# ReLU and row sum on one core: the last row in two halves instead of three pieces, and a closing wait on the two engines without work

## The chip, the core and the metric

The kernel runs on one core of a Trainium2 chip. The core has five engines that each run their own stream of instructions: TensorE (PE), VectorE (DVE), ScalarE (ACT), GpSimd (POOL) and SyncE (SP). They meet only at semaphores. SP issues the DMAs here, which 16 DMA engines carry out. The metric is the device time of one execution in microseconds (us), the median of several runs.

## The reference

The input is 32 x 512 rows of 1024 float32 numbers, 67.1 MB. Each number is clipped at zero from below, and each row is summed:

```python
def reference(x):                       # x: 32 x 512 x 1024, float32
    relu_x = np.maximum(x, 0)
    return np.sum(relu_x, axis=-1).astype(np.float32)
```

So 16,384 sums come out, 64 KB.

## The kernel before, in words

The 16,384 rows are spread over 128 partitions, 128 rows to each. The rows of the first region (112 a partition) are loaded as seven chunks of 16 rows, 8.4 MB each; the second region (16 a partition) is the tail. Three buffers of 16 rows a partition (`buf`) take the chunks in turn; the tail goes into the buffer that is next in turn. All sums gather in `res`, one column for each row of a partition.

There are two ways to take a row's sum:

- In chunks 0 to 5, ACT clips a group of 4, 5 or 7 rows in place (L119) and DVE sums that group in one reduction (L121). In chunk 5 the groups are 3, 4 and 5 rows, and the other four rows are taken in the second way.
- One instruction clips and sums a row by itself: `on_act` (L99) on ACT or `on_dve` (L102) on DVE. Each is followed by a small instruction that reads the accumulated sum out. Chunk 6 and the tail are done so, row by row in alternation, both engines at once.

SP's stream sets the order of the loads. It issues chunk after chunk (L73); from the fourth on it first waits for DVE to be done with the buffer that is to be filled. When the last buffer is free, it issues the tail without a wait in between: 8, 4, 2 and 1 rows (L79), and then the last row of each partition in three column pieces, 576, 256 and 192 wide (L87). Each load has a semaphore of its own (`s_in`). Then SP waits for the sums of chunk 6 (L90, L91) and stores the first region's 112 columns (L93). All of this is one queue in order.

The last row is summed in parts. ACT takes the 576 columns and puts their sum into an extra column at the end of the small tile `last` (L148). DVE takes the 256 columns and puts their sum into a second extra column (L150). The third piece was loaded into `last` itself, so that one pass over 194 columns, 192 of the row and the two sums, gives the row's total (L154). Ahead of it DVE waits for the third piece and for both sums (L151 to L153). SP waits for that pass, stores the last 16 columns (L158) and waits for both stores (L159, L160).

TensorE and GpSimd have no work. Their streams hold only the program's start: an opening barrier of all engines and, on GpSimd, four small fills of constants (shown as L174).

Of the kernel before, what the change touches and what calls it, by code (L numbers as in the profile page):

```python
# [2 lines left out]

P = 128
D = 1024
BIG = 16
NTWO = 6
NB = 3
REGIONS = [112, 16]
CHUNKS = [(0, 0), (0, 16), (0, 32), (0, 48), (0, 64), (0, 80), (0, 96)]  # L10
STEPS = [4, 5, 7]
MIXED = [3, 4, 5]
TAIL = [8, 4, 2, 1]
LAST = [576, 256, 192]


def bass_relu_sum_kernel(
    nc: bass.Bass,
    x: bass.AP,
    out: bass.AP,  # L20
):

    fp32 = mybir.dt.float32
    ALU = mybir.AluOpType  # L30
    AF = mybir.ActivationFunctionType
    X = mybir.AxisListType.X

    B, S, _ = x.shape
    J = B * S // P
    NBIG = len(CHUNKS)
    assert BIG * NBIG + sum(TAIL) + 1 == J == sum(REGIONS) and sum(LAST) == D

    xr = x.rearrange("b s d -> (b s) d")
    of = out.rearrange("b s -> (b s)")  # L40
    start = [sum(REGIONS[:i]) for i in range(len(REGIONS))]
    xv = [
        xr[P * s : P * (s + n), :].rearrange("(p j) d -> p j d", p=P)
        for s, n in zip(start, REGIONS)
    ]
    ov = [of[P * s : P * (s + n)].rearrange("(p j) -> p j", p=P) for s, n in zip(start, REGIONS)]

    buf = nc.alloc_sbuf_tensor("buf", [P, NB, BIG, D], fp32)
    last = nc.alloc_sbuf_tensor("last", [P, LAST[2] + 2], fp32)
    res = nc.alloc_sbuf_tensor("res", [P, J], fp32)  # L50

    n_in = NBIG + len(TAIL) + len(LAST)
    s_in = [nc.alloc_semaphore(f"s_in{i}") for i in range(n_in)]
    s_act = nc.alloc_semaphore("s_act")
    s_dve = nc.alloc_semaphore("s_dve")
    s_fact = nc.alloc_semaphore("s_fact")
    s_fdve = nc.alloc_semaphore("s_fdve")
    s_tact = nc.alloc_semaphore("s_tact")
    s_tpart = nc.alloc_semaphore("s_tpart")
    s_tdve = nc.alloc_semaphore("s_tdve")  # L60
    s_store = nc.alloc_semaphore("s_store")
    s_out = nc.alloc_semaphore("s_out")

    sp, act, dve = nc.sync, nc.scalar, nc.vector


    tb = NBIG % NB
    for c in range(NBIG + 1):
        if c >= NB:
            sp.wait_ge(s_dve, 3 * (c - NB + 1))  # L70
        if c < NBIG:
            g, j = CHUNKS[c]
            sp.dma_start(out=buf[:, c % NB, :, :], in_=xv[g][:, j : j + BIG, :]).then_inc(  # L73
                s_in[c], 16
            )
    r = 0
    tail = []
    for i, n in enumerate(TAIL):
        sp.dma_start(out=buf[:, tb, r : r + n, :], in_=xv[-1][:, r : r + n, :]).then_inc(  # L79
            s_in[NBIG + i], 16  # L80
        )
        tail.append((r, n, s_in[NBIG + i]))
        r += n
    n0, n1 = LAST[0], LAST[0] + LAST[1]
    parts = [buf[:, tb, r, 0:n0], buf[:, tb, r, n0:n1], last[:, 0 : LAST[2]]]
    for k, (lo, hi) in enumerate([(0, n0), (n0, n1), (n1, D)]):
        sp.dma_start(out=parts[k], in_=xv[-1][:, BIG - 1, lo:hi]).then_inc(  # L87
            s_in[NBIG + len(TAIL) + k], 16
        )
    sp.wait_ge(s_fact, 1)  # L90
    sp.wait_ge(s_fdve, 1)  # L91
    for g in range(len(REGIONS) - 1):
        sp.dma_start(  # L93
            out=ov[g][:, :], in_=res[:, start[g] : start[g] + REGIONS[g]]
        ).then_inc(s_store, 16)


    def on_act(t, acc):
        return act.activation(t, t, AF.Relu, accum_out=acc)  # L99

    def on_dve(t, acc):
        return dve.tensor_scalar(  # L102
            out=t, in0=t, scalar1=0.0, scalar2=None, op0=ALU.max, op1=ALU.add, accum_out=acc
        )

    def row(c, i):
        return buf[:, c % NB, i, :], res[:, c * BIG + i : c * BIG + i + 1]

    for c in range(NTWO):
        b, steps = c % NB, STEPS if c < NTWO - 1 else MIXED  # L110
        act.wait_ge(s_in[c], 16)
        if steps is MIXED:
            dve.wait_ge(s_in[c], 16)
            for i in (BIG - 4, BIG - 3):
                on_dve(*row(c, i))
        r = 0
        for i, n in enumerate(steps):
            t = buf[:, b, r : r + n, :]
            act.activation(t, t, AF.Relu).then_inc(s_act, 1)  # L119
            dve.wait_ge(s_act, 3 * c + i + 1)  # L120
            dve.tensor_reduce(  # L121
                out=res[:, c * BIG + r : c * BIG + r + n], in_=t, axis=X, op=ALU.add
            ).then_inc(s_dve, 1)
            r += n
        if steps is MIXED:
            for i in (BIG - 2, BIG - 1):
                on_act(*row(c, i))


    j0 = NBIG * BIG  # L130
    for c in range(NTWO, NBIG):
        act.wait_ge(s_in[c], 16)
        dve.wait_ge(s_in[c], 16)
        for i in range(BIG):
            ins = (on_act if i % 2 else on_dve)(*row(c, i))
            if i >= BIG - 2:
                ins.then_inc(s_fact if i % 2 else s_fdve, 1)
    for r, n, s in tail:
        if n > 1:
            act.wait_ge(s, 16)  # L140
        dve.wait_ge(s, 16)
        for i in range(r, r + n):
            f = on_act if (i - r) % 2 else on_dve
            f(buf[:, tb, i, :], res[:, j0 + i : j0 + i + 1])

    n = LAST[2]
    act.wait_ge(s_in[-3], 16)
    on_act(parts[0], last[:, n : n + 1]).then_inc(s_tact, 1)  # L148
    dve.wait_ge(s_in[-2], 16)
    on_dve(parts[1], last[:, n + 1 : n + 2]).then_inc(s_tpart, 1)  # L150
    dve.wait_ge(s_in[-1], 16)  # L151
    dve.wait_ge(s_tpart, 1)
    dve.wait_ge(s_tact, 1)  # L153
    on_dve(last[:, :], res[:, J - 1 : J]).then_inc(s_tdve, 1)  # L154


    sp.wait_ge(s_tdve, 1)
    sp.dma_start(out=ov[-1][:, :], in_=res[:, start[-1] : J]).then_inc(s_out, 16)  # L158
    sp.wait_ge(s_store, 16 * (len(REGIONS) - 1))  # L159
    sp.wait_ge(s_out, 16)  # L160


# [1 line left out]
_INS = ['x']  # L164
_OUTS = [((32, 512), 'float32')]


# [21 lines left out]
```

## Time and profile before

| | before |
|---|---|
| median of 5 runs | 161.98 us (161.84 to 162.05) |
| the profiled execution | 161.84 us |
| its span, first to last instruction | 160.5 us |
| DVE busy | 122.0 us, 76% |
| ACT busy | 101.0 us, 63% |
| POOL busy | 0.2 us; PE has no work |
| DMA, mean over the span | 419 GB/s |
| share of the chain that ended last | DMA 69%, ACT 18%, DVE 11%, SP's queue 1% |

A page of the profile shows one execution. The span is counted from the first to the last instruction of the kernel; the execution's time is longer by what lies around it. The chain of work that ended last is followed back from the last instruction, step by step, to whatever released it. In the timeline a row has its start, its duration, the engine (a q behind it means the engine's sequencer, which issues DMAs and waits), the line, the operation and the shapes; in brackets stands how long the engine had been idle before, and what ended that. The DMA issues give for each load its size and the time from the issue to its landing. Besides, the trace holds the times at which semaphores were updated, and the start, size and duration of each DMA packet.

### The profile page before, as it was taken

What the parts mean: (1) busy time and instruction counts of PE and PEld (TensorE: products, weight loads), DVE (VectorE), ACT (ScalarE), POOL (GpSimd) and SP (SyncE); (2) the same over time, 40 slices, a digit from 0 to 9 for tenths busy, and PEclk for the clock granted to TensorE, in tenths of its full rate; (3) what the DMA queues carried; (4) which work ended last, traced back from release to release, by engine and by line L of the source; (5) the groups of instructions that cost most, each with busy time, mean ns of one, the idle gap of its engine ahead of it and who ended that gap; (6) DMA issues with size and microseconds to landing.
All of it is one profiled execution on the core that took longest, in us unless ns stands there. A gap on an engine that the chain in (4) does not pass through costs nothing.

```text
span 160.5 us, 148 instructions
## 1 busy us (share of the span) xinstructions
DVE 122.0 (76%) x58; ACT 101.0 (63%) x55; POOL 0.2 (0%) x4
## 2 busy tenths in 40 slices
DVE  0000004998969898898969989699899999598995
ACT  3000039991599907997099951999329980496972
POOL 0000000000000000000000000000000000000000
DMA  7969969969969969969969969969969979799993
GB/s 261 523 278 506 523 261 523 523 261 523 523 261 523 523 261 523 523 261 523 523 261 523 523 261 523 523 261 523 506 278 523 457 327 523 343 441 388 412 402 123
DMA packets 2305, 67.18 MB, mean 419 GB/s; under 512 B 512, under 2 KB 768, under 8 KB 1024
## 3 DMA queue, kind: packets, MB, share of 16 engines
q1 hardware_dynamic: 2304, 67.18, 97.5%
q14 instruction: 1, 0.01, 0.0%
HBM read 67.11 MB, written 0.07 MB: 419 GB/s over the span
## 4 chain that ended last, share of the span: by engine, by line
DMA 69%; ACT 18%; DVE 11%; SPq 1%; issue 0%; DVEq 0%
DMA buf<-in_x_dram 69%; ACT buf L119 18%; DVE res L121 10%; DVE buf L102 1%; SPq L79 1%; SPq L73 0%; DVE last L102 0%; DVEq L153 0%
## 5 line engine op out<-in xcount | busy, mean ns | idle before, releaser
L121 DVE TENSOR_REDUCE res<-buf 128x4 f32<-128x4096 f32 (+3 forms) x18 | 100.4, 5604 | 34.2 <-ACT buf L119 34.2
L119 ACT ACTIVATE buf<-buf 128x4096 f32<-128x4096 f32 (+3 forms) x18 | 80.8, 4553 | 47.0 <-DMA buf<-in_x_dram 47.0
L99 ACT ACTIVATE buf<-buf 128x1024 f32<-128x1024 f32 (+1 forms) x18 | 18.4, 1024 | 9.8 <-DMA buf<-in_x_dram 9.8
L102 DVE TENSOR_SCALAR_CACHE_REDUCE buf<-buf 128x1024 f32<-128x1024 f32 (+1 forms) x19 | 21.3, 1174 | 2.7 <-DMA buf<-in_x_dram 2.5
L99 ACT ACTIVATION_READ_ACCUMULATOR buf<-buf 128x1 f32 x18 | 3.4, 187 | 0.0
L119 ACT ACT_TABLE_LOAD x1 | 1.3, 1283 | 0.7 <-PEq L174 0.7
L102 DVE DVE_READ_ACCUMULATOR buf<-buf 128x1 f32 x19 | 1.6, 83 | 0.0
L102 DVE TENSOR_SCALAR_CACHE_REDUCE last<-last 128x194 f32<-128x194 f32 x1 | 0.4, 355 | 0.1
L174 POOL MEMSET const-bfloat16-1.0<- 128x1 bf16 x1 | 0.1, 101 | 0.0
L174 POOL MEMSET const-uint8-127<- 128x1 uint8 x1 | 0.1, 101 | 0.0
L174 POOL MEMSET const-float32-0.0<- 128x1 f32 x1 | 0.1, 98 | 0.2 <-issue 0.2
L174 POOL MEMSET const-float32-1.0<- 128x1 f32 x1 | 0.1, 98 | 0.0
L102 DVE DVE_READ_ACCUMULATOR last<-last 128x1 f32 x1 | 0.1, 83 | 0.0
## 6 DMA issues: line engine op xcount, KB each, us to landing
buf<-in_x_dram SPq DMA_DIRECT2D x1, 4096.0 KB, 26.7
buf<-in_x_dram SPq DMA_DIRECT2D x1, 2048.0 KB, 31.2
buf<-in_x_dram SPq DMA_DIRECT2D x1, 1024.0 KB, 33.2
buf<-in_x_dram SPq DMA_DIRECT2D x1, 512.0 KB, 34.0
buf<-in_x_dram SPq DMA_DIRECT2D x1, 288.0 KB, 34.3
buf<-in_x_dram SPq DMA_DIRECT2D x1, 128.0 KB, 34.1
buf<-in_x_dram SPq DMA_DIRECT2D x7, 36.3
last<-in_x_dram SPq DMA_DIRECT2D x1, 96.0 KB, 33.9
```

Of the source, the lines that this page charges most:

```text
L79: sp.dma_start(out=buf[:, tb, r : r + n, :], in_=xv[-1][:, r : r + n, :]).then_inc(s_in[NBIG + i], 16)
L99: return act.activation(t, t, AF.Relu, accum_out=acc)
L102: return dve.tensor_scalar(out=t, in0=t, scalar1=0.0, scalar2=None, op0=ALU.max, op1=ALU.add, accum_out=acc)
L119: act.activation(t, t, AF.Relu).then_inc(s_act, 1)
L121: dve.tensor_reduce(out=res[:, c * BIG + r : c * BIG + r + n], in_=t, axis=X, op=ALU.add).then_inc(s_dve, 1)
L174: nc = _bacc.Bacc("TRN2", target_bir_lowering=False, num_devices=1)
```

## The change

The last row now arrives in two column pieces of 512 instead of three. ACT takes the first half and puts its sum behind the second half, in the one extra column of `last`; DVE's last pass goes over 513 columns. DVE's own pass over 256 columns, its sum and the semaphore `s_tpart` are gone. Of the two waits that are left ahead of the last pass, the one for ACT's sum now stands before the one for the load. At the end of their streams TensorE and GpSimd wait for the semaphore of the last load. Everything up to the last row is as it was.

```diff
-LAST = [576, 256, 192]
+LAST = [512, 512]
...
-    last = nc.alloc_sbuf_tensor("last", [P, LAST[2] + 2], fp32)
+    last = nc.alloc_sbuf_tensor("last", [P, LAST[1] + 1], fp32)
...
-    n0, n1 = LAST[0], LAST[0] + LAST[1]
-    parts = [buf[:, tb, r, 0:n0], buf[:, tb, r, n0:n1], last[:, 0 : LAST[2]]]
-    for k, (lo, hi) in enumerate([(0, n0), (n0, n1), (n1, D)]):
-        sp.dma_start(out=parts[k], in_=xv[-1][:, BIG - 1, lo:hi]).then_inc(
-            s_in[NBIG + len(TAIL) + k], 16
-        )
+    sp.dma_start(out=buf[:, tb, r, 0 : LAST[0]], in_=xv[-1][:, BIG - 1, 0 : LAST[0]]).then_inc(
+        s_in[-2], 16
+    )
+    sp.dma_start(out=last[:, 0 : LAST[1]], in_=xv[-1][:, BIG - 1, LAST[0] : D]).then_inc(
+        s_in[-1], 16
+    )
...
+    for idle in (nc.tensor, nc.gpsimd):
+        idle.wait_ge(s_in[-1], 16)
...
-    n = LAST[2]
-    act.wait_ge(s_in[-3], 16)
-    on_act(parts[0], last[:, n : n + 1]).then_inc(s_tact, 1)
-    dve.wait_ge(s_in[-2], 16)
-    on_dve(parts[1], last[:, n + 1 : n + 2]).then_inc(s_tpart, 1)
-    dve.wait_ge(s_in[-1], 16)
-    dve.wait_ge(s_tpart, 1)
-    dve.wait_ge(s_tact, 1)
+    act.wait_ge(s_in[-2], 16)
+    on_act(buf[:, tb, BIG - 1, 0 : LAST[0]], last[:, LAST[1] : LAST[1] + 1]).then_inc(s_tact, 1)
+    dve.wait_ge(s_tact, 1)
+    dve.wait_ge(s_in[-1], 16)
     on_dve(last[:, :], res[:, J - 1 : J]).then_inc(s_tdve, 1)
```

## The prediction

> **What bounds the kernel now.** I read the chain of work that ended last first, then the timeline of the last 4 us, then the DMA issues, and last the trace's record of semaphore updates and DMA packets. Times are microseconds from the span's start. The end of the chain:
>
> ```profile
> 122.91 34.02 DMA buf<-in_x_dram
> 156.93 0.02 issue
> 156.95 1.58 DVE buf L102 x4
> 158.53 0.04 DVEq L153
> 158.56 0.07 issue
> 158.63 0.36 DVE last L102 x2
> ```
>
> The reader is to see that until 156.93 the loads decide, and that the change touches only what follows. The load that lands there is row 14 of each partition. Behind it only the last row is still to come, so everything the change can win or lose in the split of that row lies in two microseconds.
>
> The timeline of that stretch (start, duration, engine, line, operation):
>
> ```profile
> 156.95 1.22 DVE L102 TENSOR_SCALAR_CACHE_REDUCE buf<-buf 128x1024 f32<-128x1024 f32 x1
> 157.69 0.68 ACT L99 ACTIVATE buf<-buf 128x576 f32<-128x576 f32 x1 [0.90 <-DMA buf<-in_x_dram]
> 158.09 0.08 DVE L102 DVE_READ_ACCUMULATOR buf<-buf 128x1 f32 x1
> 158.09 0.42 DVE L102 TENSOR_SCALAR_CACHE_REDUCE buf<-buf 128x256 f32<-128x256 f32 x1
> 158.28 0.19 ACT L99 ACTIVATION_READ_ACCUMULATOR buf<-buf 128x1 f32 x1
> 158.43 0.08 DVE L102 DVE_READ_ACCUMULATOR buf<-buf 128x1 f32 x1
> 158.63 0.35 DVE L102 TENSOR_SCALAR_CACHE_REDUCE last<-last 128x194 f32<-128x194 f32 x1
> 158.91 0.08 DVE L102 DVE_READ_ACCUMULATOR last<-last 128x1 f32 x1
> 159.03 0.34 SPq L158 DMA_DIRECT2D out_dram<-res  x1
> ```
>
> See that ACT starts its piece when the load lands, that DVE finds its 256 columns already there when row 14 is done, and that the pass over 194 columns waits for ACT's sum and its own earlier sum, not for its load. After it SP issues the last store, which takes 1.4 us to land, and the span ends at 160.49.
>
> The three loads in question, in issue order 288, 128 and 96 KB:
>
> ```profile
> buf<-in_x_dram SPq DMA_DIRECT2D x1, 288.0 KB, 34.3
> buf<-in_x_dram SPq DMA_DIRECT2D x1, 128.0 KB, 34.1
> last<-in_x_dram SPq DMA_DIRECT2D x1, 96.0 KB, 33.9
> ```
>
> With their issues at 123.40, 123.94 and 124.42 they land at 157.7, 158.1 and 158.3; the semaphore record has 157.67, 158.07 and 158.30. They were queued 34 us ahead, so it is the DMA engines' work that sets these times, not when SP issues.
>
> **The last row's loads.** Each of the 16 DMA engines carries 8 packets of each piece. The packet record gives 93 ns for 2304 B, 46 ns for 1024 B and 36 ns for 768 B. From the first two, a byte costs 47/1280 = 0.0367 ns, so a 2048 B packet is 46 + 1024 x 0.0367 = 83.6 ns (an estimate). The old row takes 8 x (93 + 46 + 36) = 1400 ns, the new 8 x 2 x 83.6 = 1338 ns, and one closing packet of 9 ns goes. So the first piece lands 8 x (93 - 83.6) = 75 ns earlier, at 157.59, and the last 71 ns earlier, at 158.23. The bounds: no gain (157.67 and 158.30), or twice the gain (157.52 and 158.16). I take the middle, worked out from the packets.
>
> The Trainium skill, "DMA: Bandwidth & Descriptors", section on the anatomy of one DMA, prices a DMA at about 2.0 us fixed plus its bytes, for the GpSimd path. Were that paid in series here, one DMA fewer would save 2 us and the kernel would come to 160; the three landings 0.40 and 0.23 us apart speak against it. Against the change speaks "Perfetto Trace Analysis", section on DMA optimizations: splitting a DMA may let some of the work start sooner where DMA engines are idle. By that rule the merge would lose the early start of the 256-column pass, 0.34, and come to 162.3; the packet record shows the engines at work on loads until 157.8, so the rule's condition isn't met here.
>
> **SP.** One issue of 0.44 us goes (three issues at L87, now two). SP stands at its wait for the big chunks' results until 147.78 anyway (the wait of 22.9 us at L91), so it saves nothing. The first store keeps its release at 147.84 and its place behind the loads in the queue.
>
> **ACT's piece.** 1024 columns take 1.06 and 576 take 0.68, which is 0.835 ns a column; 512 columns take 0.63. From start to the semaphore update the old piece took 157.69 to 158.48, 0.785; the new one 0.785 - 64 x 0.000835 = 0.73. Starting 0.02 after the landing, at 157.61 (ACT is idle from 156.79), it signals at 158.35.
>
> **DVE's last pass.** The 256-column pass and its sum go; row 14 is finished by 158.18, and DVE then waits. The new pass has 513 columns (512 and ACT's sum). In the built order a separate wait instruction holds DVE's queue for the last load, and the pass itself waits for ACT's sum; behind it stands only the pass, and SP's final store waits for that. In the trace of before, DVE's pass began 0.106 after the update that its separate wait needed (158.528 to 158.634), and 0.024 after a landing it waited for itself. So the pass begins at the later of 158.23 + 0.106 = 158.34 and 158.35 + 0.024 = 158.37. It is the second, by 0.03; if that cover went, the load would decide at nearly the same time.
>
> From a pass's start to its sum's read it is 1.145 for 1024 columns, 0.340 for 256 and 0.280 for 194. Between 256 and 1024 a column costs 1.05 ns, so 513 columns give 0.61. The read and its update took 0.095 (158.914 to 159.009). The new update comes at 158.37 + 0.61 + 0.095 = 159.08, against 159.01: **+0.07**. So 319 columns more in the last pass (+0.33) are nearly paid by its start 0.26 earlier. The 256-column pass was hidden by ACT's and is no gain in itself; its fold-in, through the wait at L153, was what held the old last pass.
>
> Bounds of this sum: with no gain at the loads ACT signals at 158.42 and the pass starts at 158.45, +0.14; if ACT's signal should also pay the slow 0.106, +0.22. With twice the gain it starts at 158.30, 0.00. The floor is DVE's own row 14: a start at 158.18 would be -0.12, for which the first piece would have to land 0.19 earlier than I say.
>
> **The idle engines' waits.** PE and POOL have one wait each as their last instruction, with nothing of the kernel behind it and no one waiting for it. They hold until 158.23. What can come late is what an engine does after its stream. The page shows none of it, but the semaphore record has one semaphore (number 2) updated at 0.94, 158.58, 158.61, 159.15 and 160.61, four more times to 160.77, then all semaphores cleared between 160.74 and 161.33, then nine more updates to 161.96. The second, fourth and fifth come 0.10 to 0.15 after ACT's, DVE's and SP's last instruction, so I read it as the engines reporting in a fixed order, PE and POOL being first and third. PE reported 0.23 after its last instruction (0.71 to 0.94). Now it would report at about 158.5, POOL with ACT at 158.6, and SP's report, the last, still comes at 160.61 + 0.07. The cover is 160.6 - 158.23, less two steps of 0.04: 2.3 us. I take a cost of 0. The bounds are below.
>
> The Trainium skill, "Runtime: NRT & Kernel Launch", section on the preamble and postamble, names a barrier of about 1.5 us for all engines and a semaphore reset of about 1.5 us after the kernel. By these figures 3 us would follow the span; the record has 0.16 from the barrier's fifth update to its ninth and 0.6 of clearing, and only 1.35 lies around the span in all, so the page's lengths are not this case's.
>
> **Sum.** The profiled execution took 161.84 with a span of 160.49, so 1.35 lies around the span and is taken as unchanged. Span 160.49 + 0.07 = 160.56, execution 161.91. The median of the five runs, 161.98, is 0.14 above that execution (the runs go from 161.84 to 162.05); the forecast is set on the median: 161.98 + 0.07 = **162.05**.
>
> **The rivals.**
> 1. *The idle engines end late* (the other side). PE or POOL needs long to get from the wait to its report, because its ending now lies at the end and not in 158 us of leisure. It decides from 2.3 us on. For it: the clearing and the second round follow only when all have reported. Against it: ACT, after waiting 20.5 us, and DVE, after 26.1 us, started 0.02 after their release; PE's longest own instruction took 0.05; the one late 8 KB instruction fetch took 0.52, and even the dearest start-up row, ACT's table load, 1.28, fits in the cover. At 3 us it would give +0.7, 162.7. Chance 0.12.
> 2. *The idle engines end better.* They reach the barrier fresh. The last group of semaphores starts to be cleared 0.19 after the ninth update, where others start 0.11 to 0.15 after theirs, and the second round starts 0.27 after the last clearing. If both went, -0.35: 161.6. Nothing in the trace ties either to how long an engine waited. Chance 0.07.
> 3. *The fold takes longer than I say*: ACT's piece lands no earlier and its signal pays 0.106. +0.22 or a little more: 162.2 to 162.3. For it: my 0.02 to 0.03 between load and signal is thin. Chance 0.09, most of it within 0.2%.
> 4. *The waits do nothing and the split breaks even*: 161.98. This lies inside the forecast's bounds.
>
> **How the numbers follow.** 0.2% is 0.32 us, about what a measurement of this kernel can tell from no change. The forecast, -0.12 to +0.22, has 0.72. Faster by over 0.2% is rival 2, 0.07; slower is rival 1 and 0.02 of rival 3, 0.14; within is 0.72 + 0.07 = 0.79. The forecast and rival 3 hold 0.81 and reach from 161.86 to 162.3; with the spread of the runs shown (about 0.1 to each side) the range is 161.80 to 162.40.
>
> **What would show it.** In the new timeline: ACT's 512-column piece at 157.6, no 256-column pass, DVE's 513-column pass from about 158.37 with its sum read at 158.98, the last store issued at 159.1, the span at 160.56. In the semaphore record the first, second and third report come between 158.4 and 158.7, the fifth near 160.7. I am wrong if the pass starts outside 158.25 to 158.55, if a report other than SP's comes last, or if the time around the span is not 1.35.

## The result, and the profile after

The changed kernel takes 162.37 us in the median (161.97 to 162.69, 23 runs) against 161.98 before (161.81 to 162.19, 43 runs). The medians differ by 0.39. The ratio is 1.0021, with a 95% interval of 1.0016 to 1.0027: slower by 0.34 us, 0.26 to 0.44. The forecast had been +0.07, within 0.2%, in a range up to 162.40.

The chain that ended last, in the changed kernel (start, duration, what):

```profile
123.58 34.20 DMA buf<-in_x_dram
157.78 0.02 issue
157.80 0.73 ACT buf L102 x2
158.53 0.03 issue
158.56 0.70 DVE last L105 x2
```

Where four DVE instructions in a row had carried the end, now ACT's half and then DVE's one long pass do. The timeline of the same stretch has the steps that were forecast (start, duration, engine, line, operation):

```profile
157.13 1.22 DVE L105 TENSOR_SCALAR_CACHE_REDUCE buf<-buf 128x1024 f32<-128x1024 f32 x1
157.80 0.63 ACT L102 ACTIVATE buf<-buf 128x512 f32<-128x512 f32 x1 [0.81 <-DMA buf<-in_x_dram]
158.28 0.08 DVE L105 DVE_READ_ACCUMULATOR buf<-buf 128x1 f32 x1
158.34 0.19 ACT L102 ACTIVATION_READ_ACCUMULATOR buf<-buf 128x1 f32 x1
158.56 0.69 DVE L105 TENSOR_SCALAR_CACHE_REDUCE last<-last 128x513 f32<-128x513 f32 x1 [0.21 <-ACT buf L102]
159.18 0.08 DVE L105 DVE_READ_ACCUMULATOR last<-last 128x1 f32 x1
159.29 0.34 SPq L157 DMA_DIRECT2D out_dram<-res  x1
```

All of it stands 0.18 later than forecast, since row 14 itself landed at 157.11 instead of 156.93. That is not the change: the first load's last part landed at 22.45 in the profile of before and at 22.51 to 22.66 in eleven of the thirteen profiles taken since; the profile of before was an early one. So the two are best laid on each other at row 14's landing. From there to the span's end it is 3.566 before and 3.638 after: **+0.07**, the forecast's sum to the hundredth. The split itself thus did in the tail what was said.

The rest of the 0.34 lies outside the span. Each execution's time less its span (spans are given to 0.1) shows it: 1.30 to 1.41 in 85 executions of the kernel before, median 1.36; 1.31 to 1.75 in 24 of the changed one, median 1.58. The profiled execution of the changed kernel is one of the cheap ones: it took 162.09, and 1.34 lie around its span, as before. So its trace shows what has changed at the end, but not the time that this costs in most executions. The page has one line of it, among the DMA queues. Before:

```profile
q1 hardware_dynamic: 2304, 67.18, 97.5%
q14 instruction: 1, 0.01, 0.0%
```

After, the part on queues has only this:

```profile
q1 hardware_dynamic: 2160, 67.18, 97.4%
```

One fetch of 8 KB of instructions is gone from it. In the trace of before it began at 160.32, 0.13 ahead of the last store's landing, and took 0.52, so that it ended beside the closing barrier, 0.35 behind the span. The trace's record of semaphore updates points to an engine. After the kernel each engine clears a group of semaphores, in five groups of about 51. The barrier goes through the engines and back; on the way back each engine updates it once more (SP with its report) and then clears. Four groups start as before, 0.11 to 0.21 after that update. The group that belongs to the second update on the way, which the report order gives to DVE, starts 0.560 after it instead of 0.145. That alone cost this execution nothing.

### The profile page after: what moved, and what is told of

The parts are those of the page before. It is cut to its first block, busy times and chain, and to the rows that moved or that the text cites. A ratio compares the mean times of both kernels' runs of the same rounds, so it can differ in the third digit from the quotient of the medians.

```text
span 160.7 us, 147 instructions
## 1 busy us (share of the span) xinstructions
DVE 122.0 (76%) x56; ACT 100.9 (63%) x55; POOL 0.2 (0%) x4
## 4 chain that ended last, share of the span: by engine, by line
DMA 69%; ACT 18%; DVE 10%; SPq 1%; issue 0%
DMA buf<-in_x_dram 69%; ACT buf L122 17%; DVE res L124 9%; SPq L79 1%; ACT buf L102 0%; DVE last L105 0%; SPq L73 0%
## 5 line engine op out<-in xcount | busy, mean ns | idle before, releaser
L105 DVE TENSOR_SCALAR_CACHE_REDUCE buf<-buf 128x1024 f32<-128x1024 f32 x18 | 21.0, 1216 | 2.7 <-DMA buf<-in_x_dram 2.5
L105 DVE TENSOR_SCALAR_CACHE_REDUCE last<-last 128x513 f32<-128x513 f32 x1 | 0.7, 689 | 0.2 <-ACT buf L102 0.2
```

The lines of the kernel that those rows point to most:

```text
L105: return dve.tensor_scalar(out=t, in0=t, scalar1=0.0, scalar2=None, op0=ALU.max, op1=ALU.add, accum_out=acc)
```

## The experiments

Theory A laid the missing 0.3 on the idle waits, B on the split, C on chance. The first four kernels take the change apart. The numbers of all twelve stand in one table at the end of this section.

**The split alone** (e1_split):

```diff
-    for idle in (nc.tensor, nc.gpsimd):
-        idle.wait_ge(s_in[-1], 16)
```

> The changed kernel without the two idle waits: only the last row's split is changed. Theory A (the last row's split costs about 0.08 us, and the rest of the change's 0.39 us comes from the idle waits, through the loads' first landings): +0.05 to +0.12 us against before, about 162.05. Theory B (the split and what goes with it, one DMA and one semaphore fewer and a wider tile, carries all of it): +0.3 to +0.4, about 162.35. Theory C (neither; the programs differ by how the loads happened to start in the runs shown): a number between -0.1 and +0.4 that does not repeat in the other kernels of this call. By every theory DVE's last pass ends about 0.08 later behind the last load's landing than before.

Measured: 162.33 against 161.94, ratio 1.0020 (1.0011 to 1.0029). Theory B's number.

**The waits alone** (e2_waits), added to the kernel before:

```diff
+    for idle in (nc.tensor, nc.gpsimd):
+        idle.wait_ge(s_in[-1], 16)
```

> The kernel before with the two idle waits added at the end of the streams of TensorE and GpSimd; the last row stays in three pieces. Theory A: +0.25 to +0.35 us, about 162.3, with a wider spread from run to run, and the slowest DMA engine's last piece of the first load landing 0.1 to 0.3 later than 22.45. Theory B: 0.0 within 0.08, about 162.0. Theory C: no fixed number. By every theory the barrier behind the kernel still waits for SP last, and about 1.35 us lies around the span.

Measured: 162.00 against 161.94, ratio 1.0004 (0.9995 to 1.0013). From row 14's landing to the span's end it is 3.567, against 3.566. Theory A falls. The end of its chain is that of before:

```profile
157.07 0.02 issue
157.09 1.58 DVE buf L105 x4
158.67 0.04 DVEq L156
158.71 0.07 issue
158.78 0.36 DVE last L105 x2
```

**The changed kernel once more** (e3_again), beside the others:

> The changed kernel once more, beside the others on one chip. Theories A and B: +0.34 us with an interval about 0.1 wide, as in the comparison shown. Theory C: any number between -0.1 and +0.4, and an order of the kernels that differs from the one shown.

Measured: 162.34, ratio 1.0023 (1.0014 to 1.0031). The difference repeats, so theory C falls.

**The idle waits on the first load** (e4_early):

```diff
     for idle in (nc.tensor, nc.gpsimd):
-        idle.wait_ge(s_in[-1], 16)
+        idle.wait_ge(s_in[0], 16)
```

> The changed kernel with the two idle waits on the first load's semaphore instead of the last one's, so that both engines end at about 22.5 us. Theory A in the form that what counts is the engines standing at a wait of the kernel while the first load starts: +0.34, as the changed kernel. Theory A in the form that what counts is their ending near the kernel's end: +0.08, as the split alone. Theory B: +0.34. Theory C: no fixed number.

Measured: 162.38, ratio 1.0023 (1.0013 to 1.0033). The first report at the barrier moves to 22.84, and the third comes 0.04 after the second again; the tail (3.638) and DVE's late clearing (0.547) stay. It is the split.

Of the split, the tail explains 0.07. In the profile of the split alone the 8 KB fetch is behind the span: asked for the stretch from the span's end on, the DMA view answers

```profile
DMA packets 1, 0.01 MB, mean 4 GB/s; under 512 B 0, under 2 KB 0, under 8 KB 0
## 3 DMA queue, kind: packets, MB, share of 16 engines
q14 instruction: 1, 0.01, 0.9%
```

The packet record puts it at 162.11, for 0.34: it begins among the last updates of the second round (161.84 to 162.20) and ends after them all, at 162.45. That led to theory D: the 256-column pass and its sum's read were two instructions of DVE's stream, and with a shorter stream a fetch that had begun just before the last store's landing is made only after the kernel. E puts it on SP's stream (one DMA fewer), F on anything else.

**Two fills ahead of the split** (e5_dve2). They change one spare column each while DVE waits for the first load:

```diff
+    for k in range(2):
+        dve.memset(pad[:, k : k + 1], 0.0)
```

> The split alone (no idle waits) with two tiny fills of a spare tile at the head of DVE's stream, while DVE waits for the first load; DVE's stream is then as long as before the change or one longer. Theory D (DVE's stream became an instruction shorter, so that the 8 KB instruction fetch which ran at 160.3, beside the last store, comes only after the kernel's end, and DVE's clearing of semaphores starts 0.4 late and the execution ends up to 0.4 later): +0.05 to +0.10 us against before, about 162.03, around the span 1.35 in every run, DVE's group of semaphores cleared from 0.15 after its barrier update, the fetch back at about 160.4. Theory E (SP's stream, one DMA shorter, is what moved): +0.34, as the split. Theory F (something else of the split): +0.34.

Measured: 162.04 against 162.00, ratio 1.0005 (0.9995 to 1.0014), around the span 1.31 to 1.39 in eleven executions. DVE's clearing starts 0.144 after its update, and the fetch is back, at 160.50:

```profile
q1 hardware_dynamic: 2160, 67.18, 97.3%
q14 instruction: 1, 0.01, 0.0%
```

Two added instructions of 59 ns each take about 0.25 off the kernel (1.0020 to 1.0005; the medians stood 0.39 above before and stand 0.04 above it). SP's stream is as short here as in the split alone, which speaks against theory E. The tail keeps its cost: 3.633.

**One fill** (e6_dve1), the same with `range(1)`:

> The same with one fill. Theory D: either as with two fills, +0.05 to +0.10, if the removed pass counts as one instruction of the stream, or as the split alone, +0.34, if it counts as two. Theories E and F: +0.34.

Measured: 162.39, ratio 1.0029 (1.0017 to 1.0040). One is not enough, so the removed pass counts as two. It is even a little worse than none (DVE's clearing starts 0.695 after its update, around the span 1.58 to 1.88), which no theory said. In its profile 0.10 of that can be seen: the second round of updates takes 0.453, where it takes 0.356 to 0.358 in the thirteen others, because the fourth update, DVE's by the order, comes 0.139 after the third and not 0.044.

**One more wait in SP's stream** (e7_sp1):

```diff
     sp.wait_ge(s_out, 16)
+    sp.wait_ge(s_in[0], 16)
```

> The split alone with one more wait at the end of SP's stream, on the first load's semaphore, which is long there; SP's stream is as long as before the change. Theory D: +0.34, around the span 1.35 to 1.73 from run to run. Theory E: +0.05 to +0.12, around the span 1.35. Theory F: +0.34.

Measured: 162.29 against 162.00, ratio 1.0012 (1.0003 to 1.0021). The profile has DVE's clearing 0.549 after its update and no fetch in the span, as in the changed kernel. The time lies between the two numbers: by the ratio +0.19, by the medians +0.29. Around the span it is 1.33 to 1.62, and in six of eleven no more than 1.42. An SP stream of the old length thus does not bring the prompt clearing back, and the two fills did so without it, so theory E falls as the cause; that SP's stream has no part in it is not shown. Why SP's wait, which lengthens the span's end by 0.07, makes the late end rarer is not settled.

**A row moved to ACT, the last row still in three pieces** (e8_row):

```diff
-            f = on_act if (i - r) % 2 else on_dve
+            f = on_act if (i - r) % 2 or (n == 8 and i == r + 6) else on_dve
```

> The kernel before, last row in three pieces, with one row of the tail's first piece (the seventh of its eight) moved from DVE to ACT. DVE's stream is then as long as in the changed kernel and ACT's one row longer; ACT's extra 1.04 us fits into its wait for the next pieces, so the last passes should stand where they stood. Theory D: the span as before within 0.05, yet +0.2 to +0.35 us, around the span 1.4 to 1.7, DVE's group cleared from 0.5 after its barrier update. Theories E and F: within 0.08 of before, around the span 1.35.

Measured: 162.24, ratio 1.0016 (1.0007 to 1.0024); from row 14's landing to the end 3.569, as before; around the span 1.49 to 1.76; DVE's clearing 0.550 after its update. So the cost appears without any split. The edit had a second effect that the expectation had not priced: ACT's stream grew by two, and ACT's group too was cleared 0.422 after its update instead of 0.114. So this run does not say which of the two streams costs; e10_row_fill2 takes them apart.

**The changed kernel whole, with two fills** (e9_after_fill2), the fills as above:

> The changed kernel whole, idle waits included, with two tiny fills at the head of DVE's stream. Theory D (the position of an instruction fetch in DVE's stream, two instructions shorter by the change): +0.05 to +0.12 us against before, about 162.05, around the span 1.30 to 1.41 in every run, an 8 KB fetch at about 160.4. Rival G (the fills helped the split alone by chance, or the idle waits put the late fetch back): +0.2 to +0.4, around the span up to 1.7.

Measured: 162.10 against 162.04, ratio 1.0004 (0.9995 to 1.0013), around the span 1.32 to 1.40. Rival G falls. From row 14's landing to the end it is 3.650. This fits the forecast's +0.07 with the late fetch taken away; the interval, -0.08 to +0.21, does not tell it from no change.

**The moved row with two fills on DVE** (e10_row_fill2):

> The kernel before with the moved row (three pieces, DVE's stream two instructions shorter) and two fills at the head of DVE's stream, so that it is as long as before. Theory D: 0.00 within 0.08, around the span 1.30 to 1.41. Rival H (the row given to ACT, whose stream grew by two, is what costs there): +0.2 to +0.3, as without the fills.

Measured: 162.19, ratio 1.0011 (1.0002 to 1.0020), around the span 1.44 to 1.63. DVE's clearing is back at 0.151 and its fetch in the span (160.62), but ACT's still starts 0.435 after its update, and one more fetch runs at 162.09. With DVE put right the time hardly falls (1.0016 to 1.0011, intervals that overlap), so rival H holds: ACT's stream alone keeps the late end. Two engines have been shown to do this, DVE and ACT; the others were not tried in this way.

**24 fills** (e11_split_fill24), the fills as above with `range(24)`:

> The split alone with 24 tiny fills at the head of DVE's stream, all done long before the first load lands. Theory D: the fetch starts earlier, where the stream passes the same place 22 instructions sooner, in the last rows at about 147 to 152; around the span 1.30 to 1.41; +0.05 to +0.12. If only one exact length were good: around the span up to 1.7, +0.34.

Measured: 162.77 against 162.04, ratio 1.0049 (1.0036 to 1.0061). Around the span it is 1.33 to 1.40 and DVE's clearing starts at 0.139; the fetch ran at 131.07, earlier than I had said. So not one exact length is good; a longer one does too. But the span grew: its mean is 161.44, against 160.68 for the kernel before beside it. The start of the timeline shows the fills beside the first loads' issues:

```profile
0.73 1.33 SPq L74 DMA_DIRECT2D buf<-in_x_dram  x3
0.80 0.71 DVE L112 MEMSET pad<- 128x1 f32 x24 [0.80 <-PEq L175]
```

The first load landed at 23.18, where most profiles have 22.5 to 22.7, and row 14 at 158.15. The packet record shows two things there. The 16 first packets took 3.20 to 4.11, against 2.42 to 3.29 before; that the fills did this was not tried. And the fetch fell among the loads: it ran from 131.07 to 131.39, the 64 KB packet that began at 131.38 took 3.08 instead of 2.42, and from then on one of the 16 parts of each load, which had been 0.09 behind the first part, lands 1.05 to 1.09 behind it. It is the last part by 0.44 to 0.48, and a load is used only when all its parts are there. By these times the fetch kept one of the DMA engines from its loads. Near the end of this kernel it cost nothing; here, amid the loads, it goes with about 0.47.

**The kernel before with its waits in another order** (e12_order):

```diff
-    dve.wait_ge(s_in[-1], 16)
     dve.wait_ge(s_tpart, 1)
     dve.wait_ge(s_tact, 1)
+    dve.wait_ge(s_in[-1], 16)
```

> The kernel before with the three waits ahead of its last pass in another order, so that the pass itself waits for DVE's own sum and the separate wait for the last load and ACT's sum. Theory of the prediction's step (0.106 from an update to the pass behind a separate wait, 0.024 where the pass waits itself): the last pass starts 0.03 instead of 0.106 after DVE's sum, so the span after the last row-14 landing is 0.05 to 0.08 shorter; about 161.90. Rival: the pass behind a separate wait needs its 0.1 whatever it waits for, no change in the trace, 161.98.

Measured: 161.98 against 162.04, ratio 0.9996 (0.9987 to 1.0005), not told apart from before. From row 14's landing to the end it is 3.541, 0.025 less; I had expected 0.05 to 0.08. The last pass did not start 0.024 after DVE's own sum (158.649) but at 158.721, which is 0.106 after ACT's (158.615): the separate wait now held ACT's sum, and that decided. The 0.106 of a separate wait stands; moving it from one late sum to another one 0.03 earlier brings only that.

| kernel | DVE, ACT records | landing of row 14 to the span's end | around the span, range (executions) | DVE's clearing after its update | fetch at |
|---|---|---|---|---|---|
| before | 61, 57 | 3.566 | 1.30 to 1.41 (85) | 0.145 | 160.32 |
| after | 59, 57 | 3.638 | 1.31 to 1.75 (24) | 0.560 | none recorded |
| e1_split | 59, 57 | 3.643 | 1.37 to 1.73 (11) | 0.554 | 162.11 |
| e2_waits | 61, 57 | 3.567 | 1.32 to 1.40 (11) | 0.151 | 160.47 |
| e3_again | 59, 57 | 3.637 | 1.32 to 1.69 (11) | 0.547 | 162.06 |
| e4_early | 59, 57 | 3.638 | 1.38 to 1.70 (8) | 0.547 | 162.05 |
| e5_dve2 | 61, 57 | 3.633 | 1.31 to 1.39 (11) | 0.144 | 160.50 |
| e6_dve1 | 60, 57 | 3.649 | 1.58 to 1.88 (6) | 0.695 | 162.32 |
| e7_sp1 | 59, 57 | 3.705 | 1.33 to 1.62 (11) | 0.549 | none recorded |
| e8_row | 59, 59 | 3.569 | 1.49 to 1.76 (11) | 0.550 | 162.02, 162.10 |
| e9_after_fill2 | 61, 57 | 3.650 | 1.32 to 1.40 (11) | 0.144 | 160.93 |
| e10_row_fill2 | 61, 59 | 3.596 | 1.44 to 1.63 (11) | 0.151 | 160.62, 162.09 |
| e11_split_fill24 | 83, 57 | 3.599 | 1.33 to 1.40 (5) | 0.139 | 131.07 |
| e12_order | 61, 57 | 3.541 | 1.31 to 1.39 (11) | 0.144 | 160.43 |

The second column counts the records of the two engines' streams in the trace. Read the columns together. Where DVE has 61 or more, its clearing is prompt and its fetch begins in the span, 1.16 to 1.20 after its report at the barrier in all six kernels with 61; with 59 or 60 the clearing is 0.4 to 0.55 late. The split has its own, separate column: 3.54 to 3.60 in three pieces, 3.63 to 3.71 in two, but for the kernel with 24 fills.

In the six profiles with a fetch after 162 the time around the span of that very execution is 1.47 to 1.69, and 1.34 to 1.35 in the eight without one. In those six the fetch's end lies 0.23 to 0.24 behind the point that the execution's time would give from the span's start. In the other eight it is the last update of the second round that lies 0.11 to 0.13 behind that point. So there the execution ends with those updates, and in the six with the fetch. The profiles of after and e7_sp1 have the late clearing without such a fetch, and no added time: the cost goes with the late fetch, not with the late clearing. In five of the six the fetch begins 0.65 to 0.70 after the late group's clearing has begun, which points to the late engine as its owner but does not show it.

## Why the prediction was right or wrong

- **The loads: right.** The 2048 B packet had been estimated at 83.6 ns; it takes 84. After row 14 the two pieces land at 0.671 and 1.338; forecast 0.67 and 1.31. The last landing gained 0.036 on before and not 0.071; over the kernels in two pieces it varies from 1.30 to 1.35.
- **ACT's piece: right.** 0.63, and its signal 1.425 after row 14; forecast 1.42.
- **DVE's last pass: right in time, and either releaser may decide.** It starts 1.457 after row 14 (forecast 1.45), the sum is read 0.61 later and signalled 0.094 after that. Both releasers came together, as the 0.03 of cover had said: the load's 0.119 and ACT's 0.032 before the start. The forecast had ACT's deciding by 0.03. It did in the profiles of e1_split and e3_again (0.024 before the start); here, by the same delays, it was the load.
- **SP: right on the span.** One issue fewer changes nothing there.
- **The idle waits: right in price, wrong in a detail.** The waits alone cost nothing that can be told (1.0004). The third report, POOL's by the order assumed, came 0.27 after the second, not 0.04, and 0.54 after POOL's wait had passed; SP's still came last, 1.46 after DVE's. Rival 2's 0.19 is 0.21 in the record (160.770 to the group's first recorded clearing at 160.984). Rivals 1 and 2 looked for the end at the engines with the waits, and neither happened. Rival 3's longer fold did not happen either.
- **"1.35 lies around the span and is taken as unchanged": wrong, and this is the step that failed.** The median of the time around the span went from 1.36 to 1.58. I had seen the 8 KB fetch at 160.32 and used it only as a price for PE. I had not asked whose it was and when it would run. Its place follows the length of DVE's stream (160.32 with 61 records, 131.07 with 83, none in the span with 59 or 60), so it was DVE's; before, it cost nothing where it ran. The change took two instructions out of DVE's stream, and I counted them as time on DVE alone. In the sum the term "around the span" was 0.00 and measured about +0.25 (the changed kernel's ratio less that with fills: 1.0021 - 1.0004, 0.28; the medians around the span, 0.22).
- **The range: held by luck.** 162.37 lies under the upper bound of 162.40, but the room up there had been given to rival 3 and to the spread of the runs, and the 0.25 came from neither. Nor did the change clearly stay within 0.2%, to which 0.79 had been given: the ratio is 1.0021, and its interval reaches to both sides of that line.
- **The signs of being wrong.** The pass began at 158.565, a hair outside 158.25 to 158.55, only because row 14 landed 0.18 late. The first three reports came at 158.72, 158.75 and 159.02 instead of 158.4 to 158.7: that shift, and POOL's 0.27. The time around the span is the sign that told, and only over many executions, since the profiled one has 1.34.
- **The median over the profile**: the forecast took the profiled execution, 161.84, as 0.14 under the median. It was an early one by its first load, and its span (160.49) was under the mean of before's spans in the three sets of runs with experiments (160.61 to 160.68). Since the sum was made as a difference and set on the median, nothing was lost by it.

What stays open: which engine makes the fetch after 162, and why it falls late in most executions but not in all; why DVE's clearing is later still with one fill than with none; why ACT's end suffers from two instructions more, and DVE's from one or two fewer; why a wait on SP makes the late end rarer; and why the first packets are slower with 24 fills.

## What to carry to other kernels

An edit that adds or drops a few instructions can move the end of an execution by 0.2 to 0.4 us without touching any busy engine: look at the time less the span in every run, and at when the instruction fetch (queue 14) runs, before a difference of that size is explained from inside the span. The page's line alone does not tell: e10_row_fill2 has it and ends late, and with 24 fills it stands there for a fetch amid the loads. Two idle instructions on the engine in question are a cheap trial; here they gave 0.25 us back. And compare two profiles from a common landing on, not from the span's start, when the loads feed everything.

## What the runs showed of the hardware that was not expected

- The start of the loads is kept to the end. The DMA engines' first packets of 64 KB took 2.4 to 3.3 us, most of them 3.0 to 3.2, and began up to 1.06 apart in the profile of before, where later packets take 2.42, and the slowest DMA engine's delay there is still there at row 14: from the first load's landing to row 14's it is 134.44 to 134.54 in thirteen of the fourteen profiles (the other is the one with 24 fills, 134.97), while the first landing itself moves from 22.45 to 23.02. Less the first landing, the spans of the profiles in three pieces are 137.99 to 138.14, and those in two, but for the 24 fills, 138.10 to 138.17. Whether it is also most of the spread from run to run (160.5 to 161.0 before) is not shown, since those runs have no trace.
- The end of the execution depends on the length of an engine's stream, as told above. The Trainium skill, "Runtime: NRT & Kernel Launch", section on instruction fetch, says that crossing a 16 KiB boundary costs one DMA tail-bump and is mostly hidden. The fetches recorded here are of 8192 B. One behind the kernel went with 0.12 to 0.34 more around the span in six profiles, and one amid the loads went with landings 0.47 later.
- An instruction behind a separate wait started 0.106 after the last semaphore of that wait, in the kernel before and with the reordered waits, and 0.119 in the changed one; an instruction that waits itself started 0.02 to 0.03 after.
